# One tile pool for the up and the down product, with the down product's two-pair step first

## The chip, the cores and the metric

The kernel runs on one core of a Trainium2 chip. The metric is the device time of one execution in microseconds; lower is better. All inputs and outputs are float32 in HBM.

## The reference

One layer of a trunk over 2048 frames of width 1024: a norm, a combined input projection, two token mixers (a gated short convolution and a Mamba-2 scan), an output projection with a residual, and then the part that this document is about, a squared-ReLU MLP with a residual, and a last norm.

```python
x = x + jnp.einsum("btc,cd->btd", y, w_out)                  # after the mixers
h = rmsnorm(x, norm_mlp_w)
hid = jnp.square(jax.nn.relu(jnp.einsum("btd,df->btf", h, w_up)))   # 1024 -> 4096
x = x + jnp.einsum("btf,fd->btd", hid, w_down)               # 4096 -> 1024
return rmsnorm(x, final_norm_w)
```

## The kernel before

**Products.** Every large product is a 2x2 block product in Winograd's form: seven products of half-size blocks in place of eight. The weight side gives four blocks and three sums of them, the data side (here the hidden activations) four blocks and three sums: `b11`, `t1`, `t2`, `b21`, `t3`, `b22`, `t4`. Each float32 operand is split into a high part (`whi`, `uh`), made by a cast on ScalarE (ACT), and a low part (`wlo`, `ul`), made by a subtraction on VectorE (DVE). A product of two blocks is then three matmuls of 128x128 weights with 512 columns: high x high, high x low, low x high (lines 276 to 278). TensorE (PE) accumulates in PSUM banks named `px`, `py` and `pw`. `pw` begins as a copy of `px` once `b11` is summed, made on ACT (line 283, the "seed copy").

**Up product.** The tokens are two halves of 1024. For each half `Mlp.half` walks 16 "pairs" of 256 hidden columns. A pair (`Mlp.pair`) is one `chain` of seven products over 4 data pairs, 84 matmuls. Its results get relu and square on ACT; then `sums` forms the three sums on DVE (the last is `t4`), and `store` writes the seven blocks to `hid_d` in HBM over the DMA queue of SyncE (SP). While one pair runs, the weights of the next are loaded (`wraw`), summed (`s12`, `s34`) and split (`split_w`, lines 100 and 101).

**Down product.** It is a row of steps (`STEPS`). A step is a list of groups (half, output block, hidden pairs), and the groups of a step share one `chain`. The groups that sum over four hidden pairs take 84 matmuls, a two-pair group takes 42. The hidden blocks must be back in SBUF and split again; they sit in `uh`/`ul` tiles in the places that the up product's data leave free. This "refresh" (`refill`) loads a block into one of four `rh` buffers (line 974), casts it on ACT (line 347) and subtracts on DVE (line 348). Before, all four hidden pairs 0 to 3 are refreshed during the seven products of the last up pair. The sums of a step are added by DVE (line 1022) into accumulator tiles `acc`, which begin as the residual `x1_d`; `outs` loads them (line 982), four for each output block.

**Pools and order.** A tile pool hands out a fixed number of buffers for each tag. The up product has a pool `up` (`utmp`, `uhid`), the down product a pool `dp` (`acc`), and `dp` is opened when `up` is closed, in the same room. So no `acc` load is issued before the last up pair has let go of its tiles. Within an engine, instructions run in the order in which they stand. That order is set when the program is built, by a scheduler that takes what is ready by priority, mostly the order of writing, and may put a later step's matmuls ahead of an earlier one's. SP issues all large DMAs in order.

Of the kernel before, what the change touches and what calls it, by code (L numbers as in the profile page):

```python
# [16 lines left out]
P = 128  # L17
T = 2048
D = 1024
# [7 lines left out]
EPS = 1e-5  # L27
FF = 4096
# [11 lines left out]
def trunk(ctx: ExitStack, tc: tile.TileContext, x, w_in, w_dt, w_out, w_up, w_down, cvec, hrow, out):  # L40
# [150 lines left out]
    class Seven:  # L191
# [19 lines left out]
        def sums(self, e0, e1, e2, t4):  # L211

            self.sub(e2[:, 0], e2[:, 1], e0[:, 1])
            self.sub(e0[:, 1], e0[:, 1], e0[:, 0])
            self.sub(e1[:, 0], e2[:, 1], e0[:, 1])
            self.sub(t4, e1[:, 1], e1[:, 0])

# [27 lines left out]
        def chain(self, groups, ws, ahead, evict, after):  # L245
# [18 lines left out]
            for name, wn, half, acc in PRODUCTS:  # L264
# [15 lines left out]
                for gi in range(len(groups)):  # L280
                    if name == "b11" and not fresh:
                        pm[gi]["w"] = bank("w")
                        nc.scalar.copy(pm[gi]["w"], pm[gi]["x"])  # L283
                        seeds.add(gi)
                    evict(name, gi, pm[gi])
# [551 lines left out]
    class Mlp(Seven):  # L837
# [15 lines left out]
        def tmp(self, name):  # L853
            return self.up.tile([P, TB], F32, tag="utmp", name=name, bufs=8)

        def wide(self, name):
            return self.up.tile([P, 2, TB], F32, tag="uhid", name=name, bufs=5)

        def store(self, h, q, e0, e1, e2):
            t4 = self.tmp("t4")  # L860
            if h == 1 and q >= LAST:
                nc.sync.dma_start(b12_d[:, q - LAST], e0[:, 1])
            self.sums(e0, e1, e2, t4)
            for i, e in enumerate((e0, e1, e2)):
                nc.sync.dma_start(hid_d[h][q][:, 2 * i : 2 * i + 2], e)
            nc.sync.dma_start(hid_d[h][q][:, 6], t4)

        def pair(self, h, q, ws, ahead, after):

            e0, e1, e2 = (self.wide(n) for n in ("e0", "e1", "e2"))  # L870
            s = {}

            def copy(pm, name):
                s[name] = self.tmp(name)
                nc.scalar.copy(s[name], pm)

            def add(o, pm, name):
                nc.vector.tensor_tensor(out=o, in0=pm, in1=s[name], op=ALU.add)

            def relu2(o, i):  # L880
                nc.scalar.activation(o, i, AF.Relu)
                nc.scalar.activation(o, o, AF.Square)

            def evict(name, gi, pm):
                if name == "b11":
                    if gi not in self.seeds:
                        copy(pm["x"], "s1")
                elif name == "t1":
                    copy(pm["y"], "s5")
                elif name == "t2":  # L890
                    copy(pm["x"], "s2")
                elif name == "b21":
                    if gi in self.seeds:
                        relu2(e0[:, 0], pm["w"])
                    else:
                        add(e0[:, 0], pm["w"], "s1")
                        relu2(e0[:, 0], e0[:, 0])
                elif name == "t3":
                    add(e2[:, 1], pm["x"], "s5")
                    relu2(e2[:, 1], e2[:, 1])  # L900
                elif name == "b22":
                    add(e0[:, 1], pm["y"], "s2")
                    relu2(e0[:, 1], e0[:, 1])
                else:
                    relu2(e1[:, 1], pm["x"])

            got = self.chain([self.places], ws, ahead, evict, after)
            self.store(h, q, e0, e1, e2)
            return got
# [6 lines left out]
        def half(self, h, ws, late):  # L916
            for q in range(NQ):
# [9 lines left out]
                if last:  # L927
                    self.new = [{} for _ in range(4)]

                def after(name):  # L930
# [6 lines left out]
                    else:  # L937
                        self.refill((0, 1, 2, 3), name)
# [24 lines left out]
        def refill(self, gs, name):  # L963

            i = {"t1": 0, "b21": 1, "b22": 2, "t4": 3}.get(name)
            if i is not None:
                self.settle([self.wides.setdefault(g, {}) for g in gs], i, self.got)
            i = {"b11": 0, "t1": 1, "b21": 2, "b22": 3}.get(name)
            if i is not None:
                n = 1 if i == 3 else 2  # L970
                self.got = []
                for g in gs:
                    t = self.raw("rh")[:, 0:n]
                    nc.sync.dma_start(t, hid_d[g // NQ][g % NQ][:, 2 * i : 2 * i + n])
                    self.got.append(t)
# [85 lines left out]
        def rest(self, ws):  # L1061
# [11 lines left out]
            sums = [self.dp.tile([P, TB], F32, tag="acc", name="facc", bufs=18) for _ in range(NBB)]  # L1073
# [34 lines left out]
        def norm_out(self, tiles, bb, ts, st, *sums):  # L1108
# [3 lines left out]
            r = st.spread()  # L1112
# [14 lines left out]
        def rstd(self, w=TB):  # L1127
            return Rstd(self.dp, lambda n: self.raw(n)[:, 0], D, w)

        def finish_first(self):  # L1130

            for bb in range(NBB):
# [8 lines left out]
                acc = self.dp.tile([P, TB], F32, tag="facc", name="facc", bufs=1)  # L1141
# [26 lines left out]
    STEPS = [[(0, 0, [0, 1, 2, 3])], [(0, 2, [0, 1])], [(0, 1, [0]), (0, 3, [0, 1, 2])]]  # L1168
# [424 lines left out]
    mlp.down(c4, ws)  # L1593
# [57 lines left out]
```

## Time and profile before

| | |
|---|---|
| runs | 2643.86, 2638.73, 2642.34 us; median 2642.34 |
| the profiled execution | 2639.26 us, span 2637.1 us from first to last instruction |
| matmuls on PE | 12056, busy 2593.2 us, 98% of the span |
| DVE, ACT busy | 1927.0 us (73%), 1454.9 us (55%) |
| mean granted clock of PE | 0.998 |
| up product's second half ends, down product begins | about 1990 us from the start |
| DMA issues of hidden blocks | 96 of 512 KB and 32 of 256 KB out, the same back |

"Busy" is time in which an engine executes; a matmul's row gives its modelled length (0.39 us), while in a full stream one starts each 0.227 us. In a timeline row, `[3.23 <-DVE acc L1022]` says that the engine stood idle for 3.23 us before this instruction and that the DVE instruction of line 1022 on tile `acc` ended that. `x3` is a count of equal instructions in one row. `SPq` and `PEld` are the queue of SP and the weight loads of PE. The granted clock is the share of full speed that PE was allowed.

### The profile page before, as it was taken

The numbers are of one execution on the slowest core, as the hardware profiler recorded it, in microseconds if no ns is written. First come the engines' busy times: TensorE is split into PE (matmuls) and PEld (weight loads), VectorE is DVE, ScalarE is ACT, GpSimd is POOL, SyncE is SP. The second block draws the span as 40 slices with busy tenths as digits, with TensorE's granted clock in tenths as the row PEclk, the third lists the DMA queues.
The fourth block names the chain that finished last, engine by engine and source line by source line (L and its number), as shares of the span: only waits on it lengthen the run. The fifth ranks groups of instructions, "written<-read, shape, count | busy, mean of one in ns | idle before, by whom it ended". The sixth has DMA issues, their size and how long they took to land.

```text
span 2637.1 us, 33648 instructions
## 1 busy us (share of the span) xinstructions
PE 2593.2 (98%) x12056; PEld 2129.4 (81%) x12056; DVE 1927.0 (73%) x2656; ACT 1454.9 (55%) x2212; POOL 55.2 (2%) x98
## 2 busy tenths in 40 slices
PE   7999999999999999999999999999999999999998
PEld 5788888788888888887888888888887888888887
DVE  7977877778778777868777765644448777888885
ACT  6654345776667676857336555655554444444443
POOL 0010000000000000000000000000000000000001
PEclk9999999999999999999999999999999999999999
DMA  3545735555555588867656786855558544665762
GB/s 146 198 175 180 278 144 195 186 172 168 171 160 177 166 274 258 271 211 231 200 197 238 273 317 220 281 205 206 185 202 284 154 153 151 214 208 179 242 204 70
DMA packets 252168, 536.96 MB, mean 204 GB/s; under 512 B 26208, under 2 KB 93024, under 8 KB 252000
## 3 DMA queue, kind: packets, MB, share of 16 engines
q1 hardware_dynamic: 252000, 534.82, 60.9%
q8 instruction: 94, 1.54, 0.2%
q14 instruction: 74, 0.61, 0.1%
HBM read 354.89 MB, written 179.83 MB: 203 GB/s over the span
## 4 chain that ended last, share of the span: by engine, by line
PE 65%; issue 24%; ACT 5%; DMA 3%; DVE 2%; POOL 0%; SPq 0%; POOLq 0%; DVEq 0%; ACTq 0%
PE px L276 9%; PE px L277 9%; PE px L278 9%; PE py L276 5%; PE py L278 5%; PE py L277 5%; PE pm L113 4%; PE pm L114 4%; PE pm L115 4%; PE pw L276 2%; PE pw L278 2%; PE pw L277 2%; DMA dec<-rd_d 1%; PE yd L1300 1%; PE yo L1297 1%
## 5 line engine op out<-in xcount | busy, mean ns | idle before, releaser
L276 PE MATMUL px<-uh,whi 128*128 128x512 f32 x1672 | 656.8, 393 | 6.4 <-DVE acc L1022 2.5
L278 PE MATMUL px<-uh,wlo 128*128 128x512 f32 x1672 | 651.7, 390 | 0.0
L277 PE MATMUL px<-ul,whi 128*128 128x512 f32 x1672 | 651.5, 390 | 0.0
L276 PEld LDWEIGHTS px<-uh,whi 128*128 128x128 f32 x1672 | 314.2, 188 | 82.4 <-DVE acc L1022 5.3
L101 DVE TENSOR_TENSOR wlo<-wraw,whi 128x1024 fp32r<-128x1024 f32 x214 | 222.8, 1041 | 202.2 <-ACT whi L100 202.2
L278 PEld LDWEIGHTS px<-uh,wlo 128*128 128x128 f32 x1672 | 314.2, 188 | 66.2 <-issue 0.2
L277 PEld LDWEIGHTS px<-ul,whi 128*128 128x128 f32 x1672 | 314.3, 188 | 63.5
L100 ACT CAST whi<-wraw 128x1024 fp32r<-128x1024 f32 x214 | 193.8, 906 | 310.9 <-PE px L277 218.1
L100 ACT CAST whi<-s 128x1024 fp32r<-128x1024 f32 x210 | 219.7, 1047 | 223.7 <-PE py L277 92.5
L276 PE MATMUL py<-uh,whi 128*128 128x512 f32 x836 | 327.6, 392 | 4.2 <-DVE acc L1022 3.2
L277 PE MATMUL py<-ul,whi 128*128 128x512 f32 x836 | 326.0, 390 | 0.0
L278 PE MATMUL py<-uh,wlo 128*128 128x512 f32 x836 | 325.7, 390 | 0.0
L101 DVE TENSOR_TENSOR wlo<-s,whi 128x1024 fp32r<-128x1024 f32 x210 | 255.4, 1217 | 75.0 <-ACT whi L100 74.0
L113 PE MATMUL pm<-uh,whi 128*128 128x512 f32 (+1 forms) x648 | 251.5, 389 | 2.1 <-ACT uh L205 2.1
L114 PE MATMUL pm<-ul,whi 128*128 128x512 f32 (+1 forms) x648 | 248.7, 384 | 0.0
L115 PE MATMUL pm<-uh,wlo 128*128 128x512 f32 (+1 forms) x648 | 248.1, 383 | 0.0
L276 PEld LDWEIGHTS py<-uh,whi 128*128 128x128 f32 x836 | 157.1, 188 | 39.1 <-DVE acc L1022 3.7
L278 PEld LDWEIGHTS py<-uh,wlo 128*128 128x128 f32 x836 | 157.1, 188 | 33.0 <-DVE wlo L101 0.2
L277 PEld LDWEIGHTS py<-ul,whi 128*128 128x128 f32 x836 | 157.0, 188 | 32.1
L347 ACT CAST uh<-rh 128x1024 fp32r<-128x1024 f32 (+1 forms) x128 | 120.3, 944 | 84.0 <-PE py L278 66.0
L276 PE MATMUL pw<-uh,whi 128*128 128x512 f32 x418 | 163.3, 391 | 0.7 <-ACT pw L283 0.7
L278 PE MATMUL pw<-uh,wlo 128*128 128x512 f32 x418 | 162.7, 389 | 0.0
(240 smaller groups left out, 3772.0 us busy)
## 6 DMA issues: line engine op xcount, KB each, us to landing
hid_d<-e SPq DMA_DIRECT2D x96, 512.0 KB, 3.8
rh<-hid_d SPq DMA_DIRECT2D x96, 512.0 KB, 4.4
wraw<-w_in SPq DMA_DIRECT2D x68, 512.0 KB, 3.9
wraw<-w_down SPq DMA_DIRECT2D x104, 256.0 KB, 3.7
wraw<-w_up SPq DMA_DIRECT2D x48, 512.0 KB, 4.2
dec<-rd_d SPq DMA_DIRECT2D x32, 512.0 KB, 5.5
wraw<-w_out SPq DMA_DIRECT2D x32, 512.0 KB, 5.1
x_d<-xt SPq DMA_DIRECT2D x64, 256.0 KB, 3.6
```

What stands on the lines that cost most here:

```text
L100: nc.scalar.copy(hi, raw)
L101: eng.tensor_tensor(out=lo, in0=raw, in1=hi.bitcast(F32), op=ALU.subtract)
L113: nc.tensor.matmul(out, whi, hi, start=(k == 0), stop=False)
L114: nc.tensor.matmul(out, whi, lo, start=False, stop=False)
L115: nc.tensor.matmul(out, wlo, hi, start=False, stop=(k == nk - 1))
L276: nc.tensor.matmul(p, hi, h[0], start=not seeded and k == 0, stop=False, **kw)
L277: nc.tensor.matmul(p, hi, h[1], start=False, stop=False, **kw)
L278: nc.tensor.matmul(p, lo, h[0], start=False, stop=(k == len(g) - 1), **kw)
L347: nc.scalar.copy(p[i][0], t)
L1297: nc.tensor.matmul(yo[:, j * L : (j + 1) * L], state[:, j * P : (j + 1) * P], cT, start=True, stop=True)
L1300: nc.tensor.matmul(yd[(i % 2) * 64 : (i % 2) * 64 + 64, (i // 2) * L : (i // 2 + 1) * L], byhead(t["xdt"])[:, i, :], t["dec"][:, i % 2 * 4 ...
```

## The change

Up and down product share one pool. The tiles of 128x512 of the up product (temporaries and hidden blocks) and the accumulators are now all of one tag, `acc`, with 18 buffers; the hidden blocks are seven single tiles in place of three double ones and a single one, and go out in seven DMAs. The first two steps of the down product change places: the two-pair step (output block 2, hidden pairs 0 and 1) comes first, the four-pair step (block 0) second. The refresh of hidden pairs 0 and 1 runs during the last up pair as before, that of pairs 2 and 3 one product later each, and its end lies in the first down step (tables `UP` and `DOWN`). The accumulators of the first step are loaded inside the last up pair, behind `b21`, those of each later step one step ahead. The seed copy gets a higher priority in the scheduler (`FIRST`).

```diff
+FIRST = 200
...
                     if name == "b11" and not fresh:
                         pm[gi]["w"] = bank("w")
-                        nc.scalar.copy(pm[gi]["w"], pm[gi]["x"])
+                        with tc.high_priority(offset=FIRST):
+                            nc.scalar.copy(pm[gi]["w"], pm[gi]["x"])
...
         def tmp(self, name):
-            return self.up.tile([P, TB], F32, tag="utmp", name=name, bufs=8)
-
-        def wide(self, name):
-            return self.up.tile([P, 2, TB], F32, tag="uhid", name=name, bufs=5)
+            return self.up.tile([P, TB], F32, tag="acc", name=name, bufs=18)
+
+        BLOCKS = ("b11", "t1", "t2", "b21", "t3", "b22", "t4")
-        def store(self, h, q, e0, e1, e2):
+        def store(self, h, q, e):
...
-            self.sums(e0, e1, e2, t4)
-            for i, e in enumerate((e0, e1, e2)):
-                nc.sync.dma_start(hid_d[h][q][:, 2 * i : 2 * i + 2], e)
-            nc.sync.dma_start(hid_d[h][q][:, 6], t4)
+            for n in ("t2", "t3", "t4"):
+                e[n] = self.tmp(n)
+            self.sub(e["t3"], e["b22"], e["t1"])
+            self.sub(e["t1"], e["t1"], e["b11"])
+            self.sub(e["t2"], e["b22"], e["t1"])
+            self.sub(e["t4"], e["b21"], e["t2"])
+            for i, n in enumerate(self.BLOCKS):
+                nc.sync.dma_start(hid_d[h][q][:, i], e[n])
...
                     if h == 0:
                         self.refresh(name)
                     else:
-                        self.refill((0, 1, 2, 3), name)
+                        self.change(self.UP, name)
...
+        UP = {
+            "b11": [("get", 0, 0), ("get", 0, 1)],
+            "t1": [("put", 0, 0), ("get", 1, 0)],
+            "b21": [("put", 1, 0), ("get", 2, 0), ("put", 0, 1), ("get", 1, 1)],
+            "b22": [("put", 2, 0), ("get", 3, 0), ("put", 1, 1), ("get", 2, 1)],
+            "t4": [("put", 3, 0), ("get", 3, 1)],
+        }
+        DOWN = {"b11": [("put", 2, 1)], "t1": [("put", 3, 1)]}
+
+        def change(self, todo, name):
+
+            for what, i, half in todo.get(name, ()):
+                getattr(self, what)((2 * half, 2 * half + 1), i)
+            if todo is self.UP and name == "b21":
+                self.acc = {}
+                self.outs(*STEPS[0][0][0:2])
...
-                t[n] = self.dp.tile([P, TB], F32, tag="acc", name="acc", bufs=18)
+                t[n] = self.tmp("acc")
...
-        def down(self, stack, ws):
-            self.dp = stack.enter_context(tc.tile_pool(name="dp", bufs=1, reuse_waits="tile"))
-            self.acc = {}
-            for d in range(4):
-                self.outs(0, d)
+        def down(self, ws):
...
+                    if n == 0:
+                        self.change(self.DOWN, name)
...
-    STEPS = [[(0, 0, [0, 1, 2, 3])], [(0, 2, [0, 1])], [(0, 1, [0]), (0, 3, [0, 1, 2])]]
+    STEPS = [[(0, 2, [0, 1])], [(0, 0, [0, 1, 2, 3])], [(0, 1, [0]), (0, 3, [0, 1, 2])]]
...
         ws = mlp.half(1, ws, iter(()))
-    mlp.down(c4, ws)
+        mlp.down(ws)
```

`get` loads a hidden block of two pairs, `put` casts and subtracts it; the first number is the stage (0 to 3), the second the half of the four pairs (0: pairs 0 and 1, 1: pairs 2 and 3). The rest of the diff passes the one pool and its `facc` tiles to the last norm.

What this does to the order of instructions shows at three places. The names carry the number of the buffer as built; numbers and line numbers differ between the two programs. `hid_d1_15` are the hidden blocks of the last up pair, `x1_d` is the residual.

SP at the hand-over, before. `wraw_17126` and `wraw_17127` are the weights of the third down step, those of the first two have been issued already:

```order
L865 DMA hid_d1_15_144<-e1_16721 128x1024
L866 DMA hid_d1_15_144<-t4_16949 128x512
L957 DMA wraw_17126<-w_down 128x384
L957 DMA wraw_17127<-w_down 128x128 x2
L957 DMA wraw_17127<-w_down 128x384
L982 DMA acc_16963<-x1_d0_77 128x512
L982 DMA acc_16965<-x1_d1_78 128x512
L982 DMA acc_16967<-x1_d1_78 128x512
L982 DMA acc_16969<-x1_d0_77 128x512
```

The same place now. `wraw_17161` is the second weight tile of the second down step (the four-pair one), whose first tile was issued ahead of the refresh; `acc_17143` to `acc_17149` are that step's accumulators:

```order
L863 DMA hid_d1_15_144<-b22_17046 128x512
L952 DMA wraw_17161<-w_down 128x512
L863 DMA hid_d1_15_144<-t1_17062 128x512
L863 DMA hid_d1_15_144<-t2_17129 128x512
L998 DMA acc_17143<-x1_d0_77 128x512
L863 DMA hid_d1_15_144<-t4_17131 128x512
L998 DMA acc_17145<-x1_d1_78 128x512
L998 DMA acc_17147<-x1_d1_78 128x512
L998 DMA acc_17149<-x1_d0_77 128x512
L952 DMA wraw_17161<-w_down 128x512
```

The first step's accumulators are gone from here (they stand higher up, among the refresh loads), and the weights of the step that runs second have come down behind the stores.

DVE at the same place, before. `t4_16949` is the last subtraction of the up product; `s12_17060` and `s34_17093` are weight sums of the second step (two pairs):

```order
L348 TENSOR_TENSOR ul3_16946<-rh_16913,uh3_16945 128x512
L209 TENSOR_TENSOR t4_16949<-e1_16721 128x512
L232 TENSOR_TENSOR s12_17060<-wraw_17011 128x256
L209 TENSOR_TENSOR s34_17093<-wraw_17010,wraw_17011 128x256
L209 TENSOR_TENSOR s12_17060<-s12_17060,wraw_17010 128x256
L209 TENSOR_TENSOR s34_17093<-wraw_17010,s12_17060 128x256
L101 TENSOR_TENSOR wlo_17064<-s12_17060,whi_17063 128x512
L101 TENSOR_TENSOR wlo_17097<-s34_17093,whi_17096 128x512
L101 TENSOR_TENSOR wlo_17114<-wraw_17011,whi_17113 128x256
L1022 TENSOR_TENSOR acc_16963<-pw_17008,acc_16963 128x512
L1022 TENSOR_TENSOR acc_16965<-py_17016,acc_16965 128x512
```

DVE now. `s12_17208` and `s34_17229` are weight sums of the four-pair step, which runs second:

```order
L343 TENSOR_TENSOR ul3_17183<-rh_17124,uh3_17182 128x512
L210 TENSOR_TENSOR t2_17129<-b22_17046,t1_17062 128x512
L343 TENSOR_TENSOR ul3_17187<-rh_17126,uh3_17186 128x512
L210 TENSOR_TENSOR t4_17131<-b21_17109,t2_17129 128x512
L1034 TENSOR_TENSOR acc_17028<-px_17151,acc_17028 128x512
L1034 TENSOR_TENSOR acc_17030<-py_17174,acc_17030 128x512
L1034 TENSOR_TENSOR acc_17143<-pw_17276,acc_17143 128x512
L1034 TENSOR_TENSOR acc_17032<-px_17151,acc_17032 128x512
L226 TENSOR_TENSOR s12_17208<-wraw_17161 128x512
L210 TENSOR_TENSOR s34_17229<-wraw_17160,wraw_17161 128x512
L210 TENSOR_TENSOR s12_17208<-s12_17208,wraw_17160 128x512
```

Additions into accumulators have moved ahead of the weight sums, and the sums behind the last subtraction are now those of the wide step.

PE where the second step's weight sum `s12` is first used, now (`whi_17211` and `wlo_17212` are its two parts, `px_17151` is the end of the first step):

```order
L271 MATMUL px_17151<-ul3_17121,whi_17112 128x512
L272 MATMUL px_17151<-uh3_17120,wlo_17113 128x512
L270 MATMUL py_17288<-uh0_16950,whi_17211 128x512
L271 MATMUL py_17288<-ul0_16951,whi_17211 128x512
L272 MATMUL py_17288<-uh0_16950,wlo_17212 128x512
```

Before, PE needs DVE's first additions here: `py_17016` goes on being summed only when DVE has read it into an accumulator. The four-pair step has come to its third weight (`whi_16887`), and the two-pair step's matmuls (`px_17117`) have been drawn forward ahead of it:

```order
L277 MATMUL px_17117<-ul1_16835,whi_17063 128x512
L278 MATMUL px_17117<-uh1_16834,wlo_17064 128x512
L276 MATMUL py_17016<-uh2_16891,whi_16887 128x512
L277 MATMUL py_17016<-ul2_16892,whi_16887 128x512
L278 MATMUL py_17016<-uh2_16891,wlo_16888 128x512
```

The place that follows the first 24 matmuls of the four-pair step is now one that reads a weight of that step.

From the first matmul after the up product's last `b22`, PE has in both programs 138 matmuls up to the end of these two steps: 126 of the steps and 12 of the up product's `t4`. The order now is 18 of the two-pair step (`b11`, `t1`, `t2`), the 12 of `t4`, 18 more of the two-pair step (`b21`, `t3`, `b22`), 24 of the four-pair step (`b11`, `b21`), the 6 of the two-pair step's own `t4`, and then `py_17288`.

More of the change, by code (lines that the diff above doesn't have):

```diff
@@ L877, in add @@
             def add(o, pm, name):
-                nc.vector.tensor_tensor(out=o, in0=pm, in1=s[name], op=ALU.add)
+                e[o] = self.tmp(o)
+                nc.vector.tensor_tensor(out=e[o], in0=pm, in1=s[name], op=ALU.add)
+                relu2(e[o], e[o])
             def relu2(o, i):
@@ L1072, in rest @@
                     tiles[d + i, bb] = self.acc[1, d][n]
-            sums = [self.dp.tile([P, TB], F32, tag="acc", name="facc", bufs=18) for _ in range(NBB)]
+            sums = [self.tmp("facc") for _ in range(NBB)]
             for bb, t0, w in ((0, 0, TB), (1, 0, TB // 2), (1, TB // 2, TB // 2)):
@@ L1111, in norm_out @@
             yield
-            r = st.spread()
+            r = st.spread(self.facc()[:, 0 : st.w])
             yield
@@ L1139, in load @@
                     return t
-                acc = self.dp.tile([P, TB], F32, tag="facc", name="facc", bufs=1)
+                acc = self.facc()
                 for d in range(0, KD, 2):
```

52 lines of the change are left out of this document (22 added, 30 removed).

## The prediction

> **What bounds the kernel now.** I read the page first (shares of engines), then the table of windows by 100 us, then the waits of PE, then the timeline around the one bad window. All numbers are of the profiled execution, in us from its start.
>
> ```profile
> PE 2593.2 (98%) x12056; PEld 2129.4 (81%) x12056; DVE 1927.0 (73%) x2656; ACT 1454.9 (55%) x2212; POOL 55.2 (2%) x98
> ...
> 1900.00:2000.00 100.00, 99.60 (x439) 82.13 (x438) 56.35 (x64) 62.27 (x90) 0.00 (x0) 1.00 0.65 224
> 2000.00:2100.00 100.00, 94.26 (x404) 76.24 (x404) 77.55 (x105) 36.66 (x45) 0.00 (x0) 0.98 0.65 210
> 2100.00:2200.00 100.00, 100.00 (x440) 82.02 (x439) 75.58 (x96) 42.56 (x48) 0.00 (x0) 1.00 0.48 148
> ```
>
> TensorE is busy 98% of the span, so a change can only win or lose what TensorE waits. Between 2000 and 2100, where the up product hands over to the down product, it loses 5.7 us and its granted clock is 0.98; the neighbours lose 0 to 0.4. That window is the only one that the change can mend. Who is waited for there:
>
> ```profile
> PE py L276 <- DVE acc L1022: 3.2, 1, 3.2
> PE px L276 <- DVE acc L1022: 2.5, 5, 1.2
> PE px L276 <- ACT pw L283: 1.1, 2, 0.9
> PE pw L276 <- ACT pw L283: 0.7, 1, 0.7
> ```
>
> ```profile
> 1987.52 0.39 PE L278 MATMUL py<-uh,wlo 128*128 128x512 f32 x1
> ...
> 1990.47 0.39 PE L276 MATMUL py<-uh,whi 128*128 128x512 f32 x1
> 1991.25 0.50 PE L276 MATMUL px<-uh,whi 128*128 128x512 f32 x1 [0.40 <-DVE e L878]
> ...
> 2003.21 0.39 PE L278 MATMUL px<-uh,wlo 128*128 128x512 f32 x1
> 2004.26 0.50 PE L276 MATMUL pw<-uh,whi 128*128 128x512 f32 x1 [0.66 <-ACT pw L283]
> ...
> 2006.41 0.50 PE L276 MATMUL py<-uh,whi 128*128 128x512 f32 x1 [0.50 <-ACT whi L100]
> ...
> 2009.07 0.39 PE L278 MATMUL px<-uh,wlo 128*128 128x512 f32 x1
> 2012.69 0.54 PE L276 MATMUL py<-uh,whi 128*128 128x512 f32 x1 [3.23 <-DVE acc L1022]
> ...
> 2014.30 0.63 PE L276 MATMUL px<-uh,whi 128*128 128x512 f32 x1
> 2014.73 0.63 PE L277 MATMUL px<-ul,whi 128*128 128x512 f32 x1
> ...
> 2017.12 0.39 PE L278 MATMUL px<-uh,wlo 128*128 128x512 f32 x1
> ```
>
> From 1987.52 to 1990.47 there are 13 matmuls, so one starts each 0.227 us. 1987.52 is the last matmul of the last `b22` of the up product. The 3.23 us are the accumulators: DVE adds into them, and their loads go out only when the up pool is closed. After that pause a matmul takes 0.43 (2014.30 to 2014.73) until about 2016.4; from 1990.47 to 2017.12 there are 84 steps, which at 0.227 are 19.1 us and took 26.65. So the hand-over loses 7.6 us: waits of 4.8, restarts, and some 1.7 for the slow clock.
>
> **The change part by part.** The built order gives what stands where. "Step A" is the two-pair step that now comes first (42 matmuls), "step B" the four-pair step behind it (84).
>
> *Accumulators ahead.* A's four loads stand inside the last up pair, so the 3.23 wait goes. The 0.40 on `e` (the up product's `t4`, which may not overwrite its bank until DVE has read `t3`) may stay or grow by some tenths; it falls ahead of the new wait found below, where TensorE has time to lose, so it costs nothing either way.
>
> *Work.* Matmuls, sums and bytes stay. The hidden blocks leave in seven DMAs of 256 KB a pair, not in four: 32 x 3 = 96 more issues. At 0.43 each (below) that is 1.3 us of SP's time in a pair that takes 84 x 0.227 = 19 us. SP has room; what it hides behind is the other 17 us. Bounds 0 to +1 over all; I take 0.
>
> *Seed copy first.* It can win only what waits for `pw`: 0.9 at most in one place. The 0.66 at 2004.26 is a chain (matmul, copy, matmul), and the order has the same neighbours again in step B (12 `px`, then `pw`). Bounds -0.9 to +0.7 (a copy put first delays a cast by one copy); I take 0, and 0.8 at step B.
>
> *The new place.* B's weights are two tiles; the second, `wraw_17161`, is loaded by two DMAs, and the second of these stands on SP behind the stores of the last up pair, its `t4` included, and three accumulator loads. So the path is: refresh of pairs 2 and 3 and the `t4` subtraction on DVE, four SP issues, a landing, three sums, a cast, matmul.
>
> ```profile
> 1976.11 4.63 DVE L348 TENSOR_TENSOR ul<-rh,uh 128x1024 fp32r<-128x1024 f32 x4 [0.82 <-ACT uh L347]
> ...
> 2004.02 0.69 DVE L209 TENSOR_TENSOR t<-e 128x512 f32<-128x512 f32 x1
> 2004.62 0.42 DVE L232 TENSOR_TENSOR s<-wraw 128x256 f32<-128x256 f32 x1
> 2004.95 0.42 DVE L209 TENSOR_TENSOR s<-wraw 128x256 f32<-128x256 f32 x1
> ```
>
> The `t4` subtraction ended at 2004.7. These rows give DVE a start each 1.13, 0.60 or 0.33 us for a width of 1024, 512 or 256. Its list from the first `ul` to that `t4`, before: 16 refresh rows, six subtractions of the up pair and 7.0 us of weights (3 x 1.13 + 6 x 0.6). Now: the same 16 and six, 2.5 of A's weights (3 x 0.6 + 2 x 0.33), 1.1 of B's, and 3 x 0.6 of additions into A's accumulators, 5.4 in all; three narrow sums stand ahead of the first `ul` and start it 0.2 later. So 2003.3 if DVE waits no longer than before. But the refresh is now a chain through a ring of four buffers, each group of loads behind the subtraction of the last:
>
> ```profile
> 1977.37 5.66 DMA rh<-hid_d
> ...
> 1983.10 1.05 ACT L347 CAST uh<-rh 128x1024 fp32r<-128x1024 f32 x1 [2.01 <-DMA rh<-hid_d]
> 1984.19 1.23 DVE L348 TENSOR_TENSOR ul<-rh,uh 128x1024 fp32r<-128x1024 f32 x1 [0.50 <-ACT uh L347]
> ```
>
> ```profile
> rh<-hid_d SPq DMA_DIRECT2D x11, 512.0 KB, 5.8
> acc<-x_d SPq DMA_DIRECT2D x16, 256.0 KB, 5.5
> ...
> wraw<-w_down SPq DMA_DIRECT2D x6, 256.0 KB, 4.4
> rh<-hid_d SPq DMA_DIRECT2D x5, 256.0 KB, 3.8
> ```
>
> (DMA view of 1970 to 2030: size, median us from issue to landing.) First load done 1983.0, cast and subtraction 2.3: 1985.4. Two more rounds of 5.8 + 2.3: 2001.6. The half-size one 3.8 + 1.3: 2006.7, its partner and `t4` 1.2: 2007.9. Between 2003.3 and 2007.9 I take 2006.0, a little nearer the chain, since DVE works in order and a late load holds up all behind it.
>
> ```profile
> 1999.13 1.28 SPq L957 DMA_DIRECT2D wraw<-w_down  x3
> ...
> 2007.56 9.77 SPq L982 DMA_DIRECT2D acc<-x_d  x16
> ```
>
> An issue costs SP 0.43 to 0.61, so store, three loads and the wanted one behind them are out at 2006.0 + 4 x 0.47 = 2007.9. It lands 4.4 (its own kind) to 5.5 (the accumulators, which it stands right behind) later; I take 5.2, nearer to these: 2013.1. One addition into B's accumulators stands ahead of the sums on DVE and waits for its own load, but that was issued earlier and lands first: 0. Three sums of 0.6 with latency, 1.9: 2015.0; the cast 1.05: 2016.0. The low half needs one more subtraction of 1.23, and only two matmuls can run meanwhile: 0.8 more.
>
> *When TensorE is there.* From 1987.75 the order has 78 matmuls up to that product of B: 17.7, and 0.8 for the seed: 2006.3. It waits 9.7 us there.
>
> *Sum.* At 2012.69 before had 54 of the 126 matmuls of its first two steps left; now at 2016.0 there are 60: (2016.0 - 2012.69) + 6 x 0.227 + 0.8 = +5.5. The next bank wait (1.2, the longest on `acc` into `px`) becomes one of 0.7 to 1.2: -0.3. The slow clock: the row at 2014.30 has it after a pause of 3.23 already, so it comes after either pause and the difference is 0, bounds -0.4 (matmuls at half clock hide part of the 0.8) to +1.7. Sum +5.2. The profiled execution took 2639.26 (span 2637.1 and 2.2 around it), so 2644.5 there; the median shown is 3.1 above it, so 2647.5.
>
> The Trainium skill (TensorE: Matmul & The Clock Gate, Part 1: The HAM clock gate) lets the clock halve after at least one idle window of about 3.4 us and return after a busy one. By it the pause of 3.23 was too short to do so for certain and one of 9.7 is long enough, so the 1.7 would be new and the sum +6.9, an estimate; the trace shows the slow clock before as well, so the +5.2 stands.
>
> **The rivals.** *Faster: B's second tile is early.* If SP gets past the stores some 9.7 us sooner, by 1996, the path ends with TensorE's arrival. Then what stays of the 7.6 is the seed (0.8), and the bank wait wins 0.3: about -7, and 2635. Against it: `t4` needs the up product's last matmuls, which in the new order end near 1994.6 and are followed by two activations and three subtractions between refresh rows. For it: the first DMA of that tile stands four stores earlier.
>
> *Within 0.2%: half hidden.* If the refresh doesn't delay DVE (2003.3) and the landing is 4.4, the sum is 5.2 - 2.7 - 0.8 = +1.7: 2644. Speaks for it that pairs 2 and 3 no longer compete with as many refresh loads.
>
> *Slower by more: two slow windows.* A pause of 9.7 followed by a second of 0.8 may leave the first stretch after it too thin to count as busy: 3.4 us more at half speed, +1.7, 2649. Against it, the start of the kernel, where a pause of 2.11 follows others, and the clock is back 3.2 us later:
>
> ```profile
> 19.91 1.65 PE L113 MATMUL pm<-uh,whi 128*128 128x512 f32 x3 [2.11 <-ACT uh L205]
> ...
> 22.21 0.63 PE L114 MATMUL pm<-ul,whi 128*128 128x512 f32 x1
> ...
> 23.06 0.39 PE L114 MATMUL pm<-ul,whi 128*128 128x512 f32 x1
> 23.29 0.39 PE L115 MATMUL pm<-uh,wlo 128*128 128x512 f32 x1
> ```
>
> *The stores cost.* A store that holds SP while a weight load stands behind it could cost a wait like the 0.40 in each of the 32 pairs: +13, 2655. Against it: the window of 1900 to 2000, all up product, loses 0.4 in all with four stores a pair, so its weights come in time with much to spare. The Trainium skill (DMA: Bandwidth & Descriptors, Anatomy of one DMA) puts about 2 us of fixed cost on each DMA, which speaks against smaller ones; by it 96 more are an estimated 192 us of queue time, beside other transfers.
>
> **How the numbers follow.** A wait at B's second tile 0.66 (above +5.3: 0.34, below: 0.32), half hidden 0.13, early 0.09, two slow windows 0.08, stores 0.04. 0.2% (5.3 us) is about what the measurement can tell from no change. Slower 0.34 + 0.08 + 0.04 = 0.46, same 0.32 + 0.13 = 0.45, faster 0.09. The likeliest case alone: 2644 to 2651 (refresh -2.7 to +1.9, landing -0.8 to +0.3, clock to +1.7). Runs of one kernel spread 2638.7 to 2643.9, which widens it; the low end reaches into the half-hidden case: 2641 to 2652.
>
> **What would show it.** Right: a wait of 7 to 11 us of `py` for ACT `whi` some 18 us after the up product's last `b22`, DVE idle before the `s12` sums for a DMA `wraw<-w_down`, no wait for `acc` over 1.5 us. Wrong: that wait under 5 us, or TensorE waiting in the up half, or a granted clock below 1 twice.

## The result, and the profile after

The changed kernel took 2656.65 us (median of four runs, 2653.50 to 2658.76) against 2641.69 for the kernel before: ratio 1.0053, 95% interval 1.0041 to 1.0066, or +15.0 us. Timed again in a second series it took 2651.13 (eight runs, 2647.72 to 2657.01) against 2642.08: ratio 1.0041, interval 1.0027 to 1.0055, or +9.0. The forecast was 2647.5 in 2641 to 2652: the side was right, the amount too small, and the first measurement lies outside the range, the second within it.

The profiled execution after took 2658.76 us, its span is 2656.3 (before: 2637.1). The page's row of TensorE, then the windows by 100 us around the hand-over (PE, PEld, DVE, ACT, POOL busy, granted clock, DMA share, GB/s):

```profile
PE 2599.0 (98%) x12056; PEld 2133.1 (80%) x12056; DVE 1930.7 (73%) x2656; ACT 1456.0 (55%) x2212; POOL 55.5 (2%) x98
```

```profile
1900.00:2000.00 100.00, 100.00 (x443) 82.81 (x442) 49.94 (x61) 56.99 (x84) 0.00 (x0) 1.00 0.62 205
2000.00:2100.00 100.00, 89.78 (x382) 71.82 (x381) 77.95 (x101) 42.89 (x54) 0.00 (x0) 0.97 0.70 223
2100.00:2200.00 100.00, 100.00 (x442) 82.53 (x441) 76.44 (x97) 42.44 (x49) 0.00 (x0) 1.00 0.48 146
```

The window that holds the hand-over now loses 10.2 us where it lost 5.7. The waits of PE (us in total, times, longest):

```profile
PE py L270 <- ACT whi L101: 8.2, 1, 8.2
PE st L114 <- ACT xtok L1288: 6.5, 3, 4.4
PE px L270 <- ACT s L871: 3.4, 2, 1.8
PE px L270 <- DVE acc L1034: 3.1, 7, 0.8
```

The first row is the wait that the prediction named, for `whi` into `py`, 8.2 us long; the 3.2 for `acc` is gone and no wait for `acc` is over 0.8. Its chain, in the timeline of after:

```profile
2017.62 0.50 PE L270 MATMUL pw<-uh,whi 128*128 128x512 f32 x1 [0.66 <-ACT pw L278]
2018.94 0.69 DVE L210 TENSOR_TENSOR t<-b,t 128x512 f32<-128x512 f32 x1
2019.66 0.32 SPq L863 DMA_DIRECT2D hid_d<-t  x1
2020.03 1.55 SPq L998 DMA_DIRECT2D acc<-x_d  x3
2021.62 0.47 SPq L952 DMA_DIRECT2D wraw<-w_down  x1
2027.13 0.69 DVE L226 TENSOR_TENSOR s<-wraw 128x512 f32<-128x512 f32 x1 [3.42 <-DMA wraw<-w_down]
2029.06 2.00 ACT L101 CAST whi<-s 128x1024 fp32r<-128x1024 f32 x2 [11.49 <-DVE s L210]
2030.16 0.80 PE L270 MATMUL py<-uh,whi 128*128 128x512 f32 x1 [8.15 <-ACT whi L101]
```

Only the rows of the chain are shown. The `t4` subtraction ends at 2019.63 on DVE, its store goes out, then three accumulator loads, and only then the last DMA of `wraw_17161`. DVE waits 3.42 us for it; the sums, the cast and the matmul follow. This is the forecast path link by link. But it is not 15 us. To see where the rest lies, three seed copies serve as landmarks, at the same place of the work in every kernel; the rows of before, then of after:

```profile
1419.53 0.57 ACT L283 COPY pw<-px 128x512 f32<-128x512 f32 x1 [1.16 <-PE px L278]
...
1936.27 0.57 ACT L283 COPY pw<-px 128x512 f32<-128x512 f32 x1 [1.16 <-PE px L278]
...
2088.57 0.57 ACT L283 COPY pw<-px 128x512 f32<-128x512 f32 x1 [2.28 <-PE px L278]
```

```profile
1430.60 0.57 ACT L278 COPY pw<-px 128x512 f32<-128x512 f32 x1 [1.16 <-PE px L272]
...
1950.25 0.57 ACT L278 COPY pw<-px 128x512 f32<-128x512 f32 x1 [1.16 <-PE px L272]
...
2106.85 0.57 ACT L278 COPY pw<-px 128x512 f32<-128x512 f32 x1 [2.28 <-PE px L272]
```

After lags 11.1 at the first, 14.0 at the second, 18.3 at the third: 11.1 up to the first up pairs, 2.9 more in the up product, 4.3 more over the hand-over. The 11.1 was a surprise, since the only part of the change that touches the mixers is the seed copy's priority. That was the first suspect, and the experiments cleared it.

### The profile page after: what moved, and what is told of

Read it like the earlier page. It is cut to its first block, busy times and chain, and to the rows that moved or that the text cites. A ratio compares the mean times of both kernels' runs of the same rounds, so it can differ in the third digit from the quotient of the medians.

```text
span 2656.3 us, 33753 instructions
## 1 busy us (share of the span) xinstructions
PE 2599.0 (98%) x12056; PEld 2133.1 (80%) x12056; DVE 1930.7 (73%) x2656; ACT 1456.0 (55%) x2212; POOL 55.5 (2%) x98
## 4 chain that ended last, share of the span: by engine, by line
PE 45%; issue 24%; DMA 4%; ACT 3%; DVE 2%; POOL 0%; SPq 0%; POOLq 0%; DVEq 0%; ACTq 0%
PE px L270 6%; PE px L272 6%; PE px L271 6%; PE pm L114 3%; PE pm L115 3%; PE pm L116 3%; PE py L270 3%; PE py L271 3%; PE py L272 3%; PE pw L270 1%; PE pw L271 1%; PE pw L272 1%; DMA dec<-rd_d 1%; PE yd L1314 1%; PE yo L1311 1%
## 5 line engine op out<-in xcount | busy, mean ns | idle before, releaser
L102 DVE TENSOR_TENSOR wlo<-wraw,whi 128x1024 fp32r<-128x1024 f32 (+1 forms) x214 | 222.8, 1041 | 193.2 <-ACT whi L101 164.2
L101 ACT CAST whi<-wraw 128x1024 fp32r<-128x1024 f32 (+1 forms) x214 | 194.0, 907 | 299.6 <-PE px L271 207.8
L101 ACT CAST whi<-s 128x1024 fp32r<-128x1024 f32 (+1 forms) x210 | 220.0, 1048 | 235.1 <-PE py L271 95.0
L102 DVE TENSOR_TENSOR wlo<-s,whi 128x1024 fp32r<-128x1024 f32 (+1 forms) x210 | 255.3, 1216 | 73.6 <-ACT whi L101 72.3
```

Of the source, the lines that this page charges most:

```text
L101: nc.scalar.copy(hi, raw)
L102: eng.tensor_tensor(out=lo, in0=raw, in1=hi.bitcast(F32), op=ALU.subtract)
```

## The experiments

Each was timed against the kernel before on the same chip. The last three columns are the lag behind the first trace of before, from one trace each: at the first landmark (near 1419), then what is added up to the second (up product) and up to the third (hand-over); "measured" is the change of the median and the interval of the ratio.

| kernel | measured | interval | to 1419 | up product | hand-over |
|---|---|---|---|---|---|
| before, second trace | +0.1 | 0.9986 to 1.0011 | +5.2 | -1.1 | -0.8 |
| before + seed priority | -0.6 | 0.9986 to 1.0008 | +2.1 | +0.5 | -1.3 |
| before + seven stores | +11.2 | 1.0034 to 1.0060 | +2.9 | +3.0 | +6.6 |
| after, first / again | +15.0 / +9.0 | 1.0041 to 1.0066 / 1.0027 to 1.0055 | +11.1 / +4.5 | +2.9 / -0.1 | +4.3 / +4.7 |
| after without priority, first / again | +10.5 / +10.3 | 1.0030 to 1.0055 / 1.0023 to 1.0048 | +6.7 / +3.9 | +2.9 / +1.4 | +5.5 / +6.0 |
| the same, weights ahead | +3.0 | 1.0007 to 1.0025 | +5.2 | +0.9 | -0.8 |
| after, weights ahead | +3.0 | 1.0000 to 1.0019 | +6.7 | +0.6 | +1.3 |
| double tiles, weights ahead | +0.9 | 0.9994 to 1.0015 | +8.1 | -1.3 | +2.7 |
| the same with priority | +1.7 | 0.9999 to 1.0016 | +3.0 | -1.4 | 0.0 |
| double tiles, old order of steps | -5.4 | 0.9972 to 0.9991 | +3.1 | -1.2 | -4.9 |

**The seed copy's priority, alone (e1).**

```diff
 # before.py
-                        nc.scalar.copy(pm[gi]["w"], pm[gi]["x"])
+                        with tc.high_priority(offset=FIRST):
+                            nc.scalar.copy(pm[gi]["w"], pm[gi]["x"])
```

> The kernel before with one part of the change alone: the high priority of the seed copy (pw<-px on ACT). Theory 1 (seed): the priority moves the copies ahead of other work of ACT in all stages; between the two traces the lag of after behind before grows by about 10 us up to 1243 us, where none of the other parts of the change has touched the code, and by about 3 in the up half. So this kernel should be 8 to 13 us above the kernel before (about 2650 to 2655), with PE waiting over 4 us for ACT xtok near 1220 us and a granted clock under 1 there. Theory 2 (the priority is innocent and the lag of the mixers has another cause, such as the addresses or the timing of transfers): within 2 us of the kernel before, and the wait for xtok under 1 us.

Measured 2640.98 against 2641.58: -0.6, ratio 0.9997. Theory 1 falls: the priority alone costs nothing that can be measured. Theory 2 missed one sign: the wait for `xtok` near 1216 was 1.65 us, where it had said under 1.

**The changed kernel without the priority (e2).** The same two lines taken out of the changed kernel.

> The changed kernel without the seed copy's priority; all else stays. Theory 1 (seed): the mixers lose nothing, what is left is the hand-over: a pause of PE of about 8 us for ACT whi at the second tile of the four-pair step, in place of the 3.2 us for acc, and two windows of half clock in place of one. That is +3 to +6 us against the kernel before (about 2645 to 2648). Theory 2 (priority innocent): as the changed kernel, +13 to +17.

Measured 2652.05, +10.5. Neither theory had this: without the priority about two thirds of the first +15 stay. Its trace lags 6.7 at the first landmark, though until the first stores of hidden blocks, near 1400, its instructions on all engines stand in the order of before, row for row. So a single trace may lag by such an amount without any cause in the program; the second trace of before, below, bears that out.

**Step B's weights ahead (e3).** As e2, and

```diff
-    nc.sync.dma_start(r[:, b, at : at + len(fs)], w_down[d, 2 * i + b, :, fs[0] : fs[-1] + 1])
+    with tc.high_priority(offset=AHEAD if step is STEPS[1] else 0):
+        nc.sync.dma_start(...)        # AHEAD = 400
```

> The changed kernel without the seed copy's priority, and with the weight loads of the four-pair down step given a higher priority, so that on SP the two DMAs of its second tile stand among the refresh loads and not behind the last up pair's stores. Theory H (the pause at the hand-over comes from that place on SP, as the prediction has it): the pause of about 8 us for ACT whi goes, at most 3 us of waits are left there; 5 to 8 us below the changed kernel without the priority, and -4 to +1 against the kernel before. Rival (the pause is set by DVE or by the landing of the transfers, wherever SP issues them): the pause stays above 5 us and the time within 2 us of the changed kernel without the priority.

Measured 2644.63: 7.4 below e2 on the same chip, within the 5 to 8 expected; against before +3.0, which is above the -4 to +1. On SP the last loads of step B's weights now go out at 1988 (one row, both DMAs of its second tile), 46 us behind the second landmark of its trace (1942.33) where it was 71 in after (2021.62 and 1950.25), and the pause is gone from the waits of PE between 1990 and 2054:

```profile
1988.18 0.81 SPq L952 DMA_DIRECT2D wraw<-w_down  x2
```

```profile
1999.95 0.50 PE L270 MATMUL px<-uh,whi 128*128 128x512 f32 x1 [0.69 <-DVE b L874]
2007.34 0.50 PE L272 MATMUL px<-uh,wlo 128*128 128x512 f32 x1 [0.96 <-DVE wlo L102]
2011.12 0.50 PE L270 MATMUL px<-uh,whi 128*128 128x512 f32 x1 [0.76 <-ACT pw L277]
2051.10 0.77 PE L270 MATMUL px<-uh,whi 128*128 128x512 f32 x1 [2.91 <-DVE acc L1036]
```

Theory H holds: the place on SP was the cause. The four waits are still 5.3 us together, where at most 3 were expected. The longest is for a bank that DVE has to clear first, 2.91 us at 2051.

**Seven stores a pair, alone (e4).**

```diff
 # before.py
-                nc.sync.dma_start(hid_d[h][q][:, 2 * i : 2 * i + 2], e)
+                for j in range(2):
+                    nc.sync.dma_start(hid_d[h][q][:, 2 * i + j], e[:, j])
```

> The kernel before with seven stores of 256 KB for each up pair in place of three of 512 KB and one of 256 KB; tiles and order are untouched. Theory 1: SP has room in the up half, so within 1 us of the kernel before. Rival (the stores cost: each pair loses some tenths of a us behind 96 more issues): +3 to +13, with PE waiting in the up half.

Measured 2652.82, +11.2: the rival was right about the size, and wrong about the way. The waits of PE over 1 us between 1250 and 2050:

```profile
1405.81 0.50 PE L276 MATMUL px<-uh,whi 128*128 128x512 f32 x1 [1.33 <-ACT s L876]
...
1697.12 0.50 PE L276 MATMUL px<-uh,whi 128*128 128x512 f32 x1 [2.66 <-ACT pw L283]
...
2006.97 0.79 PE L276 MATMUL px<-uh,whi 128*128 128x512 f32 x1 [3.72 <-ACT pw L283]
2024.91 0.80 PE L276 MATMUL py<-uh,whi 128*128 128x512 f32 x1 [3.97 <-DVE acc L1023]
```

There is no wait pair by pair: from 1740 to 1940 TensorE is busy 100.00 of each 100 us. The last is the old wait for the accumulators, 3.97 where it was 3.23; the other three are for ACT, at the beginning of the up product's halves and where the down product's data are refreshed. ACT near 1695, in the second trace of before and then with seven stores:

```profile
1692.75 0.62 ACT L100 CAST whi<-a 128x512 fp32r<-128x512 f32 x1
1693.26 1.06 ACT L347 CAST uh<-rb 128x1024 fp32r<-128x1024 f32 x1
1694.22 0.58 ACT L283 COPY pw<-px 128x512 f32<-128x512 f32 x1
1694.73 1.57 ACT L347 CAST uh<-rb 128x1024 fp32r<-128x1024 f32 x2
```

```profile
1693.46 1.05 ACT L347 CAST uh<-rb 128x1024 fp32r<-128x1024 f32 x1 [0.46 <-DMA rb<-hn_d]
1694.41 0.63 ACT L883 ACTIVATE e<-e 128x512 f32<-128x512 f32 x1
1694.94 0.60 ACT L100 CAST whi<-a 128x512 fp32r<-128x512 f32 x1
1695.45 1.13 ACT L347 CAST uh<-rb 128x512 fp32r<-128x512 f32 x2
1696.49 0.58 ACT L283 COPY pw<-px 128x512 f32<-128x512 f32 x1
```

The edit changes nothing but stores on SP, but the scheduler, with other stores to place, put the refill's casts ahead of the seed copy: one wide and two narrow `uh<-rb` casts that stood behind it now stand in front (e3 and the second trace of e2 have the same), and one of the casts waits 0.46 for its load. So here the stores cost mostly through the order of ACT. At 2006.97 the copy starts at 2006.34, straight behind two narrow `uh<-rh` casts; but ACT also stood 2.35 us for a refresh load at 1997.74, so order and loads are not told apart there.

```profile
2005.30 1.13 ACT L347 CAST uh<-rh 128x512 fp32r<-128x512 f32 x2
2006.34 0.58 ACT L283 COPY pw<-px 128x512 f32<-128x512 f32 x1
```

Near 1406 it is PE's own order that changed: in all six traces with four stores a pair, three `pw` matmuls (3 x 0.227 = 0.68 us) stand between the last `py` and the matmul that waits, and in all seven with seven stores they stand behind it, so they no longer fill the wait.

**The changed kernel and its twin without the priority again, and before again.**

> The changed kernel once more, beside the changed kernel without the priority on the same chip. The priority alone, in the kernel before, moved nothing (-0.6 us), while the changed kernel stood 4.6 above its twin without the priority, on another chip. Theory P (the priority costs in company of the other parts): 4 to 6 us above the twin. Theory N (that was the spread of runs, and the 7 us by which its one trace lagged before the up product are of that execution): within 2 us of the twin, about 2652 to 2655, and the lag at the end of the mixers (1243 us) not 10 us but 2 to 7, as in the traces of the other kernels, whose mixers are instruction for instruction those of before.

> The changed kernel without the priority once more, as the twin of the run beside it: about 2652, +9 to +11 against the kernel before by either theory.

> The kernel before, for a second trace: how far two executions of the same instructions lie apart at 902, 1243, 1419 and 1990 us. If a single trace can lag 5 us in the mixers by chance, it shows here as +2 to +6 against the first trace, with the slow clock or a wait for xtok of another length near 1220 us.

Measured 2651.13 and 2652.40, side by side: theory N. The priority is worth nothing here either, and the 4.6 between them was spread. After lags 4.5 at the first landmark this time (11.1 before), and the second trace of before lags its own first by 5.2. Before's first trace, on which the prediction was made, is the earliest at that landmark of all thirteen. The hand-over is the same in all four traces of the two kernels, +4.3 to +6.0.

**Four stores again, with the rest of the change (e5).** Double tiles of one tag, nine buffers, hold the hidden blocks, the temporaries and two accumulators each; else as e3.

```diff
-            return self.up.tile([P, TB], F32, tag="acc", name=name, bufs=18)
+            t = self.up.tile([P, 2, TB], F32, tag="acc", name=name, bufs=9)
...
-            for i, n in enumerate(self.BLOCKS):
-                nc.sync.dma_start(hid_d[h][q][:, i], e[n])
+            for i, t in enumerate((e["e0"][0], e1, e2)):
+                nc.sync.dma_start(hid_d[h][q][:, 2 * i : 2 * i + 2], t)
+            nc.sync.dma_start(hid_d[h][q][:, 6], e["t4"])
```

> The changed kernel without the priority, with the weights of the four-pair step ahead, and with the hidden blocks again in double tiles (9 double buffers for all, the accumulators two to a tile), so that they leave in four stores a pair as before. Theory S (the 3 us that are left with the weights ahead are the 96 more stores: the waits of 1.4 us for ACT s near 1408 and of 2.3 for pw near 1697): these waits fall under 1 us, and the time is 2 to 4 us below that with seven stores, -2 to +1 against the kernel before. Rival (they come from the reordered steps or the shared buffers): the time stays at +2 to +4.

Measured 2643.00 against 2642.08, +0.9. The wait near 1406 is 0.73 and the one near 1697 is gone, as theory S has it. By time alone the 2 us below e3 are within the two intervals; the waits tell them apart. The double tiles also pair the buffers in another way, so e5 alone doesn't single out the stores; e4 does. At the hand-over a new wait came up, here in the PE and ACT rows:

```profile
1998.10 1.04 ACT L341 CAST uh<-rh 128x1024 fp32r<-128x1024 f32 x1 [3.02 <-DMA rh<-hid_d]
...
2001.99 0.57 ACT L277 COPY pw<-px 128x512 f32<-128x512 f32 x1
...
2002.61 0.80 PE L270 MATMUL px<-uh,whi 128*128 128x512 f32 x1 [5.25 <-ACT pw L277]
```

**The priority where a copy is stuck (e6).** e5 with the seed copy's priority.

> The kernel with double tiles (four stores a pair, weights ahead) and the seed copy's priority again. In its twin without the priority PE stood 5.3 us near 2002 for the seed copy, which ACT had behind casts of refreshed blocks that were still to land. Theory: with the priority the copy stands ahead of those casts, the wait falls to 1 us or less, and the time is 3 to 5 us below the twin: -5 to -1 against the kernel before. Rival (ACT only waits one cast later): within 1.5 us of the twin.

The wait of 5.25 becomes 0.98, as expected, but the median is 2643.53, +1.7, where -5 to -1 was expected: no less than e5, so the gain isn't kept. What stands at the end of the hand-over now is the bank wait, 2.90 where e5 had 1.59:

```profile
1993.28 0.50 PE L271 MATMUL px<-uh,whi 128*128 128x512 f32 x1 [0.98 <-ACT pw L279]
...
2047.51 0.47 PE L271 MATMUL px<-uh,whi 128*128 128x512 f32 x1 [2.90 <-DVE acc L1053]
```

The traces put this hand-over 2.7 us below that of e5, the medians don't (they were timed on different chips, with intervals of 2.2 to 2.8 us to either side): whether the priority wins anything there stays open.

**The change with the one repair (e7).** after with `AHEAD` as in e3, priority kept.

> The changed kernel with one edit: the weight loads of the four-pair step get a higher priority, so that its second tile is loaded among the refresh and not behind the last pair's stores. The seed copy's priority stays. Theory: the pause of 8 us goes and with it 6 to 8 us, as it did without the priority: +1 to +5 against the kernel before. What is left is the waits near 1406 and 1697, where the up product's halves begin. Rival (the priority brings the pause back elsewhere): +7 or more.

Measured 2644.90, +3.0, as e3. The rival falls.

**The old order of steps, with early accumulators (e8).** e5 with the four-pair step first and all four pairs refreshed in the last up pair, as before; the weights of the second and third step ahead.

```diff
-    STEPS = [[(0, 2, [0, 1])], [(0, 0, [0, 1, 2, 3])], ...]
+    STEPS = [[(0, 0, [0, 1, 2, 3])], [(0, 2, [0, 1])], ...]
-            "t1": [("put", 0, 0), ("get", 1, 0)],
+            "t1": [("put", 0, 0), ("put", 0, 1), ("get", 1, 0), ("get", 1, 1)],
...
-        DOWN = {"b11": [("put", 2, 1)], "t1": [("put", 3, 1)]}
+        DOWN = {}
...
+                            with tc.high_priority(offset=200 if step in STEPS[1:3] else 0):
```

> The four-pair step first again and all four pairs refreshed in the last up pair, as before; kept of the change are the shared pool (in double tiles, four stores a pair) and the first step's accumulators loaded inside the last up pair; the weight loads of the second and third step get a higher priority. No seed priority. Theory (the swap of the steps isn't needed, the early accumulators are the part that wins): the wait of 3.2 us for acc and the slow clock behind it go, the hand-over loses under 3 us in place of 7.6: -6 to -2 against the kernel before. Rival (the loads that go out earlier delay the refresh by as much): -1 to +2.

Measured 2636.50 against 2641.88: -5.4, ratio 0.9981, interval 0.9972 to 0.9991. It beats both kernels. In all of 1985 to 2100 one wait is over 0.2 us, and the granted clock stays at 1.00 (windows of the hand-over, then that wait):

```profile
2000.00:2010.00 10.00, 9.82 (x43) 7.61 (x41) 7.65 (x13) 6.82 (x11) 0.00 (x0) 1.00 0.88 300
2010.00:2020.00 10.00, 9.82 (x43) 7.75 (x43) 9.15 (x16) 3.71 (x5) 0.00 (x0) 1.00 0.83 287
```

```profile
2044.49 0.47 PE L270 MATMUL px<-uh,whi 128*128 128x512 f32 x1 [1.72 <-DVE acc L1051]
```

The wait of 3.23 and the slow clock behind it (1.7 in the prediction) are gone: together 4.9, as much as the hand-over wins against the first trace of before. e8 also has the double tiles and the weights ahead, so what the early accumulators give by themselves was not measured. Swapping the steps isn't needed for the gain. That the swap was what made step B's weights late is likely by the order, but not shown: every run with the late load also has seven stores a pair.

## Why the prediction was right or wrong

**The new place: right, and the right size.** The wait came where it was put, and the time over the hand-over is +4.3 to +6.0 in the four traces with it, +5.2 forecast. Set from TensorE's arrival (2006.3 forecast, 2022.0 in the trace: 15.7 later), the links compare so:

| link | forecast + 15.7 | measured |
|---|---|---|
| `t4` subtraction ends | 2021.7 | 2019.6 |
| the wanted DMA is out | 2023.6 | 2022.1 |
| it has landed, sums begin | 2028.8 | 2027.1 |
| cast begins | 2030.7 | 2029.1 |
| matmul | 2031.7 | 2030.2 |

The wait was 8.15 (8.44 in the second trace) for 9.7, and the difference is the `t4` subtraction, which ended 2.1 earlier, less 0.6 more for SP. The refresh chain, of which the prediction took a little more than the middle, delayed DVE less; and behind the subtraction the prediction names five issues but reckons four (4 x 0.47 = 1.9), where the five took 2.5. The landing was 5.0 for 5.2, sums 1.9 for 1.9, cast 1.1 for 1.0. That the place on SP is the cause, and not the landing or DVE, is shown by e3 and e7: issuing the two DMAs earlier took 7.4 us away (e3 against e2, on one chip) and 6.0 (e7 against the second series of after, each against its own before).

**Accumulators ahead: right.** The 3.23 went (no wait for `acc` over 0.8 in after). In e8, where nothing takes its place, the time is 5.4 below before, though e8 changes more than the accumulators.

**Seed copy, "I take 0": right.** -0.6 alone, and 1.3 below its twin in the changed kernel, both within the spread; the 0.66 at step B stands in the trace.

**Slow clock, "the difference is 0": right in size, though the clock did something else than thought.** After shows two windows at half speed here, the second trace three, before one:

```profile
2022.00:2027.00 5.00, 0.00 (x1) 0.00 (x0) 1.29 (x2) 0.00 (x0) 0.00 (x0) 0.99 0.98 266
2027.00:2030.20 3.20, 0.04 (x1) 0.04 (x1) 2.65 (x5) 1.14 (x2) 0.00 (x0) 0.50 1.04 398
2030.20:2033.70 3.50, 3.46 (x7) 2.28 (x8) 2.90 (x3) 1.38 (x2) 0.00 (x0) 0.50 1.07 360
2033.70:2037.00 3.30, 3.30 (x16) 2.68 (x15) 1.82 (x2) 1.05 (x1) 0.00 (x0) 1.00 0.94 290
```

The first falls into the pause and costs nothing; TensorE works 3.5 us at half speed (4.3 in the second trace), before it worked 3.4. The loss is half of that, 1.8 to 2.2 for 1.7. So the rival with two slow windows had their number in the first trace, but not their cost. By the rule of the Trainium skill (TensorE: Matmul & The Clock Gate, Part 1: The HAM clock gate) that the clock halves after an idle window of about 3.4 us, the prediction had estimated +1.7 here; the traces give +0.1 to +0.5, since the clock was slow before too.

**Work, "Bounds 0 to +1 over all; I take 0": this step failed.** The cost was priced as time of SP, 96 issues of 0.43 beside much room, and in the middle of a half SP had that room (e4: nothing lost from 1740 to 1940). What was not asked is what the scheduler does with the other engines' order when the stores change. All seven traces with seven stores show the two waits at the beginning of the up product's halves, and the six with four stores don't:

| place | seven stores | four stores |
|---|---|---|
| near 1406, for ACT `s` | 1.33 to 1.88 | 0.32 to 0.73 |
| near 1697, for ACT `pw` or `s` | 1.02 to 2.66 | 0 to 0.92 |

Means of the table of landmarks: up product +1.7 for seven stores (seven traces), -0.8 for four (six): 2.4 us; the wait near 1406, which lies ahead of the first landmark, 1.6 for 0.55: 1.0. So the term was about +3.4, not 0, with a spread of single traces of 1 to 2 us around each mean. The trace of after had said so in the forecast's own terms: of its signs of an error, TensorE waits in the up half (1.6 at 1414, 1.8 at 1709) and a granted clock below 1 more than once both came. The rival "the stores cost" had the cause, but looked for it as a wait in each of 32 pairs; the window of 1900 to 2000, which spoke against it, lies in the middle of a half and couldn't show it. e4 shows that the stores alone do it, and with four stores again (e5) the two waits are as before. Most of e4's 11.2 lies at its hand-over (+6.6, where the three traces with the old hand-over and four stores have -0.7 in the mean) and is not in this term. The 192 us of queue time that the prediction estimated from the Trainium skill (DMA: Bandwidth & Descriptors, Anatomy of one DMA) go by a fixed cost that this section states for DMAs issued by GpSimd; here SP issues them, and e4 with 96 more took 11.2 us more.

**The sum.** 5.8 over the hand-over (mean +5.1 of the four traces with the late weights, -0.7 of the three with the old hand-over), 2.4 and 1.0: 9.2, against +9.0 measured the second time and +10.5 and +10.3 for the twin. With 3.4 in place of 0, the forecast's +5.2 would have been +8.6. How much of the 5.8 the seven stores have a part in was not tried: no run has the swapped steps and the late weights with four stores a pair.

**The range failed too.** The forecast leant on one trace and three runs. Two executions of the same instructions lay 5.2 us apart at 1419 (before) and 6.6 apart (after), which is as much as the forecast effect. What in the mixers makes this isn't settled; the waits for `xtok` near 1220, where one trace of after has 4.37 and the twelve others 0 to 2.8, are a part in some traces, though the second trace of before lags without one. Nor is it settled why all four first runs of after lay at 2653.5 to 2658.8, when seven of the eight later ones lay at 2653.6 or below. About 6 of the first +15 have no cause that was found in the program. That the second series, 2651.13, falls inside the range is luck: its upper end was made of refresh, landing and clock, and what came on top was none of these.

## What to carry to other kernels

Before a step is swapped on an engine that issues in order, follow what stands behind each of its loads on that queue: here one weight load behind a store made a wait of 8 us, and issuing it earlier gave 6 to 7 us back. An edit of one engine's work can cost on another, since a scheduler that orders by readiness reorders all of them; compare the built orders at every place where buffers are refilled, not only at the place that the edit is about. And before a lag in one trace is explained, look at a second trace of the same program.

## What the runs showed of the hardware

**The clock halves after pauses of very different length.** In after it was at 0.50 from 1709.43 to 1712.85, behind a wait of 1.79:

```profile
1708.93 0.50 PE L270 MATMUL px<-uh,whi 128*128 128x512 f32 x1 [1.79 <-ACT s L871]
```

```profile
1706.02:1709.43 3.41, 1.62 (x7) 1.03 (x7) 1.54 (x3) 1.63 (x5) 0.00 (x0) 1.00 0.98 337
1709.43:1712.85 3.42, 3.42 (x9) 2.69 (x9) 1.23 (x1) 1.61 (x2) 0.00 (x0) 0.50 0.89 317
```

With the wait of 2.66 near 1697 in e4, 2.33 in e3 and 2.28 in the twin's second trace the clock stayed at 1.00. The windows of e4:

```profile
1692.11:1695.52 3.41, 2.35 (x11) 1.61 (x9) 3.41 (x5) 2.95 (x6) 0.00 (x0) 1.00 0.90 284
1695.52:1698.94 3.42, 1.82 (x8) 1.52 (x9) 2.36 (x5) 2.50 (x6) 0.00 (x0) 1.00 0.94 305
```

The Trainium skill (TensorE: Matmul & The Clock Gate, Part 1: The HAM clock gate) has it halve after at least one idle window of about 3.4 us; here 1.79 was enough once and 2.66 was not.

The traces show what decides. In each trace the slow stretches begin and end on one grid of steps of 3.41 us: they last one step in before, one or two in after, three in its second trace, and the three slow stretches of after, from 1221.33, 1709.43 and 2026.88, begin 143 and 93 steps apart. What counts is how long TensorE stands idle within one step. The 1.79 lie in one step; the 2.66 of e4 are split over two, 1.1 and 1.6, as the two windows above show (3.41 less the busy time). From 60 to 2600 us in the thirteen traces, each of the 21 steps at full clock in which TensorE was idle for 1.76 us or more was followed by a slow one; of the others, idle for up to 1.72, one was (idle for 1.50, in the second trace of before). So about half a step is enough. In a slow step 0.78 idle was enough for the next to be slow too, and 0.44 was not. This is why the same wait of 2.90 gave one slow step in e6, where it lies in one step, and two in e7, where it is split into 2.12 and 0.78, and why 8.15 gave two and 8.44 three.
